# A hybrid attention and RG-LRU block on one core: the first round of attention scores moved into the last product of the input projection, the second unit's q loaded a round later

## The chip, the core and the metric

One core of one Trainium2 chip. The metric is device time in microseconds (us). The kernel before was run three times without a profile: median 2137.27 us, from 2135.4 to 2137.36. One more execution was profiled; the trace and all times inside the kernel come from it, counted from the start of its span.

## The reference, cut to what matters

A decoder block on x of 2048 positions by 1024 features, in float32. One input projection gives q, k and v for three head groups of eight heads, two SiLU gates, the RG-LRU input and two merge gates:

```python
proj = x @ w_in[l] + b_in[l]
q, k, v, g_attn, u_lru, g_lru, gate_logits = jnp.split(proj, SPLIT_POINTS, axis=-1)
```

The attention is banded: blocks of 128 queries against their own and the previous block of keys, the positions taken with stride 1, 4 or 16 by head group. For each block:

```python
s = jnp.einsum('brnqhd,brnkhd->brnhqk', qb, kw) * (Dh ** -0.5)
s = jnp.where(valid[None, None, :, None], s, NEG_INF)
m = jnp.max(s, axis=-1, keepdims=True)
p = jnp.exp(s - m)
l = jnp.sum(p, axis=-1, keepdims=True)
o = jnp.einsum('brnhqk,brnkhd->brnqhd', p, vw)
```

The three groups are combined by their denominators. The second branch is a causal convolution and a gated linear recurrence. Both are projected, weighted with sigmoid gates, summed, projected again and layer-normed with x.

## The kernel before, in words

The kernel has three stages. The change is at the seam of the first two.

**Stage A, the input projection.** Its work is a list of steps `plan`, each a pair of 128 output features over half of the positions. A step is seven products of the Strassen kind (eight for the first step); a product is twelve 128x512 matmuls that sum up in one PSUM bank, since each float32 operand is split into a high and a low part and three of the four part products are taken (`product`, L582). The loop at L898 numbers the products T. In each turn it lets `product` issue its matmuls, runs the events due at T, the `late` queue and the chains (short sequences of follow-up work, each with a lag and costs), and then `evacuate` takes the product out of its bank. Halfway through a product, after six matmuls, `run(pe_late)` (L600) issues TensorE work that others have put off. The last step is a pair of merge gates. Each of its totals starts an `mg_chain` (L369): ScalarE takes tanh in place of the tile y (L374) and issues its store to `mg_scr` from its own DMA queue (L376). A chain started in one turn gets to its tanh in the next turn, or in the loop behind the last turn (L917).

PSUM in stage A is pool `ps`: four banks of tag q for products, two of tag t for transposes of v, two of tag g for the recurrence gates. The operand blocks of x lie in the SBUF slots X0 to X5 (`XSLOT`, L117); T4, the operand of the last but two of the products, lies in X0.

**Stage B, the attention.** Twelve units, each two heads of one group, are worked in four rounds each, so 48 rounds i. Unit u needs a tile A of q (high and low part, two loads of 1 MB), a tile B of k (two loads of 512 KB, then split in parts by another engine) and, by group, a tile V of v (four loads of 512 KB). Unit 1's q, tile A1, lies in X0, where T4 was. Loads are issued by SyncE in the order in which the program writes them. For the first units this is done during the last products (L909 to L911: unit 0's k, unit 0's q, unit 1's k, `firstv` for V00, unit 1's q), then V20 and the whole of unit 2 (L1087), then by rounds (L1095 to L1101, two pieces a round).

A round i of the loop at L1091 issues: `scores(i)` (L952, 24 matmuls on 64 rows each, pairs side by side, into four banks of tag s); `peak` (L978, VectorE adds the mask and takes the extreme of each row); `expo` (L987, ScalarE's exponential in place, with the row sums); `turn` (L993, transposes of the probabilities of round i-1) and `bring` (L1003, their copies out of PSUM into tiles ptb, half by ScalarE and half by VectorE); `values` (L1018, of round i-2, TensorE) and `leave` (L1032, of round i-3, VectorE). Each engine works in the order written. Part of round i's exponentials are issued in round i+1.

**Stage C** has the two branch projections, the merge, the output projection and the norm.

**DMA semaphores.** The DMAs of SyncE and ScalarE together take eight completion semaphores in turn, DMAHW0 to DMAHW7. A DMA that takes one up waits on its own engine's queue for the DMA that had it before to land. Tiles of stage B lie where tiles of stage A lay, and the first to write there waits for those to be done with.

Of the kernel before, what the change touches and what calls it, by code (L numbers as in the profile page):

```python
# [8 lines left out]
F32 = mybir.dt.float32  # L9
# [22 lines left out]
def hybrid_block_kernel(ctx: ExitStack, tc: tile.TileContext, a: dict, out: bass.AP):  # L32
# [135 lines left out]
    def spend(**eng):  # L168
        for k, v in eng.items():
            left[k] = left.get(k, 0.0) - v  # L170
# [590 lines left out]
    def unit(u):  # L761

        return (0, 2, 1)[u % 3], u // 3

    def unit_parts(u):

        qs, ks = USLOT[u % 3]
        g, hp = unit(u)
        q = {n: qk_scr[n, 4 * g + hp] for n in ("qh", "ql", "k")}
        units[u] = [None, None]  # L770

        def k_part(j):
# [12 lines left out]
            def fn():  # L785
                if j == 0:
                    units[u][1] = big(ks, [P, 2, S], F32R, f"B{u}")
                sp.dma_start(flat(units[u][1][:, 1, cols]), q["k"][:, cols])
                for i in range(2):
                    c0 = (2 * j + i) * CH  # L790
                    later(3 + i if u < 2 else 1, lambda c0=c0: split(slice(c0, c0 + CH)))
            return fn

        def q_part(i, n):
            def fn():
                if i == 0:
                    units[u][0] = big(qs, [P, 2, S], F32R, f"A{u}")
                sp.dma_start(flat(units[u][0][:, i]), q[n])
            return fn

        return [k_part(0), k_part(1), q_part(0, "qh"), q_part(1, "ql")]
# [3 lines left out]
    def v_parts(g, j):  # L805
        src = v_scr[g][j]

        def part(i):
            def fn():
                if i == 0:  # L810
                    VT[g, j] = big(VSLOT[g, j], [P, 16, 256], F32, f"V{g}{j}")
                V = VT[g, j]
                if g == 0:
                    sp.dma_start(V[:, 4 * i:4 * i + 4], src[i * CH:(i + 1) * CH].rearrange("(n p) f -> p n f", p=P))
                elif g == 1:
                    sp.dma_start(V[:, 4 * i:4 * i + 4], src[i * CH:(i + 1) * CH].rearrange("(j r) f -> j r f", r=4))
                else:
                    sp.dma_start(V[:, 4 * i:4 * i + 4], src.rearrange("(i r) f -> i r f", r=16)[:, 4 * i:4 * i + 4])
            return fn

        return [part(i) for i in range(4)]
# [70 lines left out]
            at(t, lambda n=n, kk=kk: comb_part(n, kk))  # L892
    at(10, lambda: start_chain(scales()))

    first, second, third, firstv = unit_parts(0), unit_parts(1), unit_parts(2), v_parts(0, 0)
    low = NS
    where = [(s, j) for s in range(NQ) for j in range(ticks[s])]
    for T, (s, j) in enumerate(where):  # L898
        now["n"] = T
        for k in ("PE", "ACT", "DVE", "POOL"):  # L900
            left[k] = min(left[k], 0.0) + LEN
        if plan[s][2]:
            spend(**COST[plan[s][2][j]])
        product(s, j)
        for fn in events.pop(T, []):
            fn()
        run(late)
        run_chains()
        if s == NQ - 1:  # L909
            for fn in ((), first[:2], first[2:], second[:2], firstv, second[2:], ())[j]:  # L910
                fn()  # L911
        evacuate(s, j)
        low = min(low, len(vacant))
        if TRACE:
            print(T, s, j, plan[s][4], len(vacant), len(lo_vacant), len(chains), {k: round(v, 1) for k, v in left.items()})
# [17 lines left out]
    at_p = stB.enter_context(tc.tile_pool(name="at_p", bufs=2, reuse_waits="tile"))  # L933
    Y = stB.enter_context(tc.tile_pool(name="Y", bufs=1, reuse_waits="tile"))
    aps = stB.enter_context(tc.tile_pool(name="aps", bufs=2, space=PSUM, reuse_waits="tile"))
    def prev(g, n):
        if g == 0:
            return n - 1 if n >= 1 else None
        if g == 1:
            return n - 4 if n >= 4 else None  # L940
        return None

    st = {}

    sta, ot = {}, {}

    def first(i, j):
        u, q = divmod(i, 4)
        g, _ = unit(u)
        return 0 if prev(g, 4 * q + j) is not None else P  # L950

    def scores(i):  # L952
        u, q = divmod(i, 4)
        g, _ = unit(u)
        A, B = units[u]
        if q == 0:
            sta[u] = p_p.tile([P, 16, 4], F32, tag="sta", name=f"sta{u}", bufs=3)
            ot[u] = at_p.tile([P, S], F32, tag="ot", name=f"ot{u}")
        for w in range(2):
            s = st["s", i, w] = [aps.tile([P, 2, 256], F32, tag="s", name=f"s{i}{w}{h}", bufs=4) for h in range(2)]  # L960
            for j in range(2):
                n = 4 * q + 2 * w + j
                lo = first(i, 2 * w + j)
                for x, y in ((0, 0), (1, 0), (0, 1)):
                    for h, hs in enumerate(HALF):
                        K = B[hs, y]
                        if g == 2:
                            k = K.rearrange("p (c r j) -> p r c j", c=4, r=16)[:, n]
                        elif lo:
                            k = K[:, n * P:(n + 1) * P]  # L970
                        elif g == 0:
                            k = K[:, (n - 1) * P:(n + 1) * P]
                        else:
                            c, r = divmod(n, 4)
                            k = K[:, (c - 1) * CH:(c + 1) * CH].rearrange("p (c r j) -> p r c j", c=2, r=4)[:, r]
                        pe.matmul(s[h][:, j, lo:256], A[hs, x, n * P:(n + 1) * P], k, start=(x + y == 0), stop=(y == 1))  # L976

    def peak(i, j, h):  # L978
        u, q = divmod(i, 4)
        lo = first(i, j)  # L980
        if h == 0:
            st["p", i, j] = p_p.tile([P, 2, 256], F32, tag="p", name=f"p{i}{j}")
        dve.tensor_tensor_reduce(out=st["p", i, j][:, h, lo:256], in0=st["s", i, j // 2][h][:, j % 2, lo:256],  # L983
                                 in1=mask[:, lo:256], scale=1.0, scalar=3e38, op0=ALU.add, op1=ALU.min,
                                 accum_out=sta[u][:, 4 * q + j, h:h + 1])

    def expo(i, j, h):  # L987
        u, q = divmod(i, 4)
        p = st["p", i, j][:, h, first(i, j):256]
        s = sta[u][:, 4 * q + j]  # L990
        act.activation(p, p, AF.Exp, scale=-1.0, bias=s[:, h:h + 1], accum_out=s[:, 2 + h:3 + h])  # L991

    def turn(i, w):  # L993
        js = (2 * w, 2 * w + 1)
        pp = [st.pop(("p", i, j)) for j in js]
# [94 lines left out]
    loads = []  # L1090
    for i in range(NG + 3):  # L1091
        u = i // 4
        on, turns = i < NG, 0 < i <= NG
        run(late)
        if i in VORD:  # L1095
            loads += v_parts(*VORD[i])
        if i % 4 == 0 and 1 <= u <= 9:
            loads += unit_parts(u + 2)
        for _ in range(2):
            if loads:  # L1100
                loads.pop(0)()  # L1101
        if on:
            scores(i)
        if i > 2:
            leave(i - 3)
        if turns:
            expo(i - 1, 2, 1)
            expo(i - 1, 3, 0)
            expo(i - 1, 3, 1)
        if on:  # L1110
            peak(i, 0, 0)
            expo(i, 0, 0)
            for j, h in ((0, 1), (1, 0), (1, 1)):
                peak(i, j, h)
        if turns:
            turn(i - 1, 0)
            bring(i - 1, 0, 0, act)
            bring(i - 1, 0, 1, dve)
        if on:
            for j, h in ((0, 1), (1, 0), (1, 1)):  # L1120
                expo(i, j, h)
            peak(i, 2, 0)
            peak(i, 2, 1)
        if turns:
            turn(i - 1, 1)
            light = unit((i - 1) // 4)[0] == 2 or i % 3 == 0
            bring(i - 1, 1, 0, dve if light else act)
        if on:
            peak(i, 3, 0)
            peak(i, 3, 1)  # L1130
            expo(i, 2, 0)
        if turns:
            bring(i - 1, 1, 1, dve)
        if i > 1 and i - 2 < NG:
            values(i - 2)
        if i in (40, 41):
            prep_wl(i - 40, 2)
# [384 lines left out]
```

## Time and profile before

| | us |
|---|---|
| three runs, median | 2137.27 |
| the profiled execution, its own time | 2143.06 |
| its span | 2141.3 |
| TensorE busy | 2101.0 (98%) |
| VectorE busy | 1700.2 (79%) |
| ScalarE busy | 1080.3 (50%) |
| last product starts | 1463.28 |
| first score matmul | 1466.09 |
| first matmul of `values(0)` | 1477.81 |
| first matmul of `scores(4)` (unit 1) | 1485.85 |

The profiled execution's own time is 1.8 us over its span, and 5.8 us over the median of the runs. PE is TensorE, PEld its weight loads, DVE VectorE, ACT ScalarE, POOL GpSimd, SP SyncE; a q behind an engine is its sequencer, which issues DMAs. A row such as `q<-xB,hS` names what is written and read, with buffer numbers left out. A wait is put down to what ended last before the instruction went on.

### The profile page before, as it was taken

Reading aid. Unit: us, or ns where it says so; the run is one execution under the profiler, and the core shown is the slowest. Engines: PE = TensorE matmul, PEld = TensorE weight load, DVE = VectorE, ACT = ScalarE, POOL = GpSimd, SP = SyncE. Lnnn points to the kernel's source line nnn. Section 1 sums busy time; section 2 is a strip of 40 time slices with the busy share of each in tenths; the row PEclk is TensorE's granted clock in tenths of the full one; section 3 lists DMA queues with packets and bytes.
Section 4 is the critical chain, followed back from the end, with each engine's and each line's share of the span. In section 5 each row is a group of like instructions: output and inputs, shape, how many; then the busy total and the mean of one; then the engine's idle time right before and its main releaser. Section 6 shows DMA issues by size and latency. Waiting matters only on the chain.

```text
span 2141.3 us, 36029 instructions
## 1 busy us (share of the span) xinstructions
PE 2101.0 (98%) x12016; PEld 1749.0 (82%) x12016; DVE 1700.2 (79%) x3009; ACT 1080.3 (50%) x2284; POOL 736.5 (34%) x581
## 2 busy tenths in 40 slices
PE   8999999999999999999999999999999999999998
PEld 6888887888888788888888887888888888878887
DVE  8788988999979977787787886886999645466667
ACT  6354545457446565546557666557999411121100
POOL 1545454554654312121222221222535434322120
PEclk9999999999999999999999999999999999999999
DMA  8888887998998977777778788779898788874431
GB/s 269 257 261 251 255 255 224 270 280 245 286 270 251 302 228 203 227 221 218 248 244 276 254 260 253 241 229 373 303 305 254 219 275 280 283 251 160 165 108 69
DMA packets 348266, 525.74 MB, mean 246 GB/s; under 512 B 123568, under 2 KB 156336, under 8 KB 344240
## 3 DMA queue, kind: packets, MB, share of 16 engines
q1 hardware_dynamic: 330368, 491.64, 71.0%
q0 software_dynamic: 10080, 18.35, 5.4%
q10 hardware_dynamic: 7632, 13.44, 1.8%
q8 instruction: 96, 1.57, 0.3%
q14 instruction: 90, 0.74, 0.1%
HBM read 318.18 MB, written 190.45 MB: 238 GB/s over the span
## 4 chain that ended last, share of the span: by engine, by line
PE 82%; ACT 6%; DMA 5%; DVE 5%; issue 1%; SPq 1%; POOL 0%; DVEq 0%; ACTq 0%; POOLq 0%
PE q L597 59%; ACT p L991 4%; PE z L1388 3%; PE z L1386 3%; PE z L1387 3%; PE yb L1276 2%; PE yb L1277 2%; PE yb L1278 2%; PE o L1029 1%; PE ya L1354 1%; PE ya L1355 1%; PE ya L1356 1%; PE vtp L348 1%; ACT ptb L1014 1%; DMA yb_scr<-gB 1%
## 5 line engine op out<-in xcount | busy, mean ns | idle before, releaser
L597 PE MATMUL q<-xT,hS 128*128 128x512 f32 x1680 | 519.0, 390 | 0.4 <-DVE y L216 0.4
L597 PE MATMUL q<-xT,l 128*128 128x512 f32 x1120 | 436.0, 389 | 0.0
L597 PE MATMUL q<-xB,hA 128*128 128x512 f32 x1248 | 389.0, 393 | 6.0 <-ACT xB L204 5.7
L597 PEld LDWEIGHTS q<-xT,hS 128*128 128x128 f32 x1680 | 314.1, 188 | 65.4 <-issue 0.8
L597 PE MATMUL q<-xB,l 128*128 128x512 f32 x904 | 354.8, 392 | 1.9 <-DMA l<-wl_scr 1.8
L597 PEld LDWEIGHTS q<-xB,hA 128*128 128x128 f32 x1248 | 235.0, 189 | 56.1 <-ACT xB L204 5.7
L597 PEld LDWEIGHTS q<-xT,l 128*128 128x128 f32 x1120 | 210.2, 188 | 44.0
L597 PEld LDWEIGHTS q<-xB,l 128*128 128x128 f32 x904 | 171.1, 189 | 39.4 <-DMA l<-wl_scr 2.7
L216 POOL TENSOR_TENSOR S<-S,wA 128x512 f32<-128x512 f32 x35 | 45.7, 1305 | 418.9 <-DVE S L216 328.4
L216 POOL TENSOR_TENSOR sw<-sw,sin 128x512 f32<-128x512 f32 x96 | 160.7, 1679 | 72.0 <-DMA sw<-y 59.4
L261 ACT ACTIVATE hA<-wA 128x512 fp32r<-128x512 f32 x218 | 135.7, 624 | 90.3 <-DMA wA<-in_w_in_dram 43.0
L597 PE MATMUL q<-xB,hS 128*128 128x512 f32 x560 | 175.6, 395 | 3.0 <-DVE v L216 3.0
L991 ACT ACTIVATE p<-p,sta 128x256 f32<-128x256 f32 (+1 forms) x384 | 172.2, 455 | 5.9 <-DVE sta L983 5.2
L597 PE MATMUL q<-xT,hA 128*128 128x512 f32 x560 | 173.0, 390 | 1.5 <-DVE xT L205 0.9
L261 ACT ACTIVATE hS<-S 128x512 fp32r<-128x512 f32 x175 | 109.1, 623 | 99.2 <-DVE S L216 54.6
L216 POOL TENSOR_TENSOR l<-wA,hA 128x512 fp32r<-128x512 f32 x68 | 104.9, 1543 | 83.0 <-ACT hA L261 66.5
L597 PEld LDWEIGHTS q<-xB,hS 128*128 128x128 f32 x560 | 105.1, 190 | 25.0 <-issue 3.8
L597 PEld LDWEIGHTS q<-xT,hA 128*128 128x128 f32 x560 | 104.8, 188 | 24.6 <-DVE xT L205 1.3
L983 DVE CUSTOM_DVE_ANT_0 p<-s,mask 128x256 f32<-128x256 f32 (+1 forms) x384 | 118.7, 360 | 4.7 <-PE s L976 3.7
L216 DVE TENSOR_TENSOR y<-y,cos 128x512 f32<-128x512 f32 x96 | 108.8, 1139 | 14.8 <-DMA sw<-y 14.6
L1360 POOL TENSOR_TENSOR me<-gA,ybr 128x512 f32<-128x512 f32 x32 | 49.9, 1573 | 181.2 <-DVE gA L1359 119.6
L1388 PE MATMUL z<-wo,ml 128*128 128x512 f32 (+1 forms) x264 | 101.2, 383 | 0.9 <-DVE ml L1373 0.8
(201 smaller groups left out, 4423.7 us busy)
## 6 DMA issues: line engine op xcount, KB each, us to landing
wA<-in_w_in_dram SPq DMA_DIRECT2D x253, 256.0 KB, 5.0
wl_scr<-l SPq DMA_DIRECT2D x105, 512.0 KB, 4.9
l<-wl_scr SPq DMA_DIRECT2D x105, 512.0 KB, 4.8
sw<-y SPq DMA_DIRECT2D x384, 64.0 KB, 3.0
wS<-in_w_in_dram SPq DMA_DIRECT2D x70, 256.0 KB, 4.5
wS<-in_w_in_dram POOLq DMA_DIRECT2D x70, 256.0 KB, 6.3
qh_scr<-hi SPq DMA_DIRECT2D x48, 256.0 KB, 5.2
v_scr<-vs SPq DMA_DIRECT2D x48, 256.0 KB, 4.4
```

The lines of the kernel that those rows point to most:

```text
L216: eng.tensor_tensor(out=out, in0=in0, in1=in1, op=op)
L261: act.activation(h, r, AF.Copy)
L597: pe.matmul(bank, w[:, ks], x[:, kk, xx], start=(first and i == 0), stop=(last and i == 11))
L983: dve.tensor_tensor_reduce(out=st["p", i, j][:, h, lo:256], in0=st["s", i, j // 2][h][:, j % 2, lo:256], in1=mask[:, lo:256], scale=1.0, s ...
L991: act.activation(p, p, AF.Exp, scale=-1.0, bias=s[:, h:h + 1], accum_out=s[:, 2 + h:3 + h])
L1276: pe.matmul(yb, WL[f][:, 0, k], xx[:, 0], start=(k == 0), stop=False)
L1277: pe.matmul(yb, WL[f][:, 0, k], xx[:, 1], start=False, stop=False)
L1278: pe.matmul(yb, WL[f][:, 1, k], xx[:, 0], start=False, stop=(k == 7))
L1360: pool.tensor_tensor(out=ME[c][:, f], in0=ga, in1=yb, op=ALU.add)
L1386: pe.matmul(z, mh[:, k], w[:, 0, hs], start=(k == 0), stop=False)
L1387: pe.matmul(z, mh[:, k], w[:, 1, hs], start=False, stop=False)
L1388: pe.matmul(z, ml[:, k], w[:, 0, hs], start=False, stop=(k == 7))
```

## The change

`scores`, `peak`, `expo` and what they need are moved, as they are, ahead of the loop of stage A, with three differences for round 0. Its scores go into the banks of tags t and g of `ps`. Its probabilities are one tile p0 in slot X0, behind T4. Its row extremes and sums, sta0, are a tile of the constants' pool. `scores(0)` is put into the last product's `run(pe_late)`, and `first_round`, all eight peaks and exponentials of round 0, is issued right behind that product, ahead of that turn's chains. Stage B's loop starts its own scores at round 1. Unit 1's q can now be loaded into X0 only when round 0's probabilities have been transposed, and is issued near the end of round 1 in the program.

```diff
-    first, second, third, firstv = unit_parts(0), unit_parts(1), unit_parts(2), v_parts(0, 0)
+    st = {}
+    sta, ot = {}, {}
...
+    def scores(i):
+        u, q = divmod(i, 4)
+        g, _ = unit(u)
+        A, B = units[u]
+        if i == 0:
+            sta[u] = cst.tile([P, 16, 4], F32, name="sta0")
+            p0 = big("X0", [P, 4, 2, 256], F32, "p0")
+            for j in range(4):
+                st["p", i, j] = p0[:, j]
+        elif q == 0:
+            sta[u] = p_p.tile([P, 16, 4], F32, tag="sta", name=f"sta{u}", bufs=3)
+        for w in range(2):
+            if i:
+                s = [aps.tile([P, 2, 256], F32, tag="s", name=f"s{i}{w}{h}", bufs=4) for h in range(2)]
+            else:
+                s = [ps.tile([P, 2, 256], F32, tag="tg"[w], name=f"s{i}{w}{h}", bufs=2) for h in range(2)]
...
+    def first_round():
+        for j in range(4):
+            for h in range(2):
+                peak(0, j, h)
+                expo(0, j, h)
+
+    early_k, late_k, third, firstv = unit_parts(0), unit_parts(1), unit_parts(2), v_parts(0, 0)
...
+        if T == len(where) - 1:
+            pe_later(0, lambda: scores(0))
         product(s, j)
+        if T == len(where) - 1:
+            first_round()
...
-            for fn in ((), first[:2], first[2:], second[:2], firstv, second[2:], ())[j]:
+            for fn in ((), early_k[:2], early_k[2:], late_k[:2], firstv, (), ())[j]:
...
-        on, turns = i < NG, 0 < i <= NG
+        on, turns = 0 < i < NG, 0 < i <= NG
...
-        if turns:
+        if i > 1 and turns:
             expo(i - 1, 2, 1)
             expo(i - 1, 3, 0)
             expo(i - 1, 3, 1)
...
+        if i == 1:
+            for fn in late_k[2:]:
+                fn()
```

The order of SyncE's DMAs from V00 to V10, with the semaphores that each waits for. Before:

```order
L814 DMA V00_14283<-v_scr00_75 128x4x256 [waits DMAHW6_49]
L798 DMA A1_14309<-qh_scr8_105 128x2048 [waits DMAHW7_49,PE_49]
L798 DMA A1_14309<-ql_scr8_106 128x2048 [waits DMAHW0_49]
L818 DMA V20_14356<-v_scr20_79 128x1024 [waits DVE_49,DMAHW1_49,PE_49,Activation_49]
L818 DMA V20_14356<-v_scr20_79 128x1024 [waits DMAHW2_49]
L818 DMA V20_14356<-v_scr20_79 128x1024 [waits DMAHW3_49]
L818 DMA V20_14356<-v_scr20_79 128x1024 [waits DMAHW4_49]
L788 DMA B2_14361<-k_scr4_95 128x1024 [waits DMAHW5_49]
L788 DMA B2_14361<-k_scr4_95 128x1024 [waits DMAHW6_49]
L798 DMA A2_14364<-qh_scr4_93 128x2048 [waits DMAHW7_49,PE_49,Pool_49]
L798 DMA A2_14364<-ql_scr4_94 128x2048 [waits DMAHW0_49]
L816 DMA V10_14422<-v_scr10_77 128x1024 [waits DMAHW1_49]
```

And in the changed kernel, from B2's second half on:

```order
L788 DMA B2_14404<-k_scr4_95 128x1024 [waits DMAHW4_49]
L798 DMA A2_14407<-qh_scr4_93 128x2048 [waits DMAHW5_49,PE_49,Pool_49]
L798 DMA A2_14407<-ql_scr4_94 128x2048 [waits DMAHW6_49]
L816 DMA V10_14419<-v_scr10_77 128x1024 [waits DMAHW7_49]
L816 DMA V10_14419<-v_scr10_77 128x1024 [waits DMAHW0_49]
L798 DMA A1_14505<-qh_scr8_105 128x2048 [waits DMAHW1_49,PE_49,Activation_49]
L798 DMA A1_14505<-ql_scr8_106 128x2048 [waits DMAHW2_49]
L816 DMA V10_14419<-v_scr10_77 128x1024 [waits DMAHW3_49]
```

A1's two loads have moved from ahead of V20 to behind V20, B2, A2 and the first two parts of V10. A2's two loads now wait for the semaphores that the last two gate stores hold, as the next rows show.

ScalarE at the seam: y71_3 and y63_3 are the last two gate tiles, p the probabilities, ptb01 the copy of the second half of round 0's transposes. Before:

```order
L374 ACTIVATE y71_3_14312<-y71_3_14312,bh_195 128x512 [waits DVE_49]
L376 DMA mg_scr_73<-y71_3_14312 128x512 [waits DMAHW2_49,Activation_49]
L374 ACTIVATE y63_3_14334<-y63_3_14334,bh_195 128x512 [waits DVE_49]
L376 DMA mg_scr_73<-y63_3_14334 128x512 [waits DMAHW5_49,Activation_49]
L991 ACTIVATE p00_14397,sta0_14367<-p00_14397,sta0_14367 128x128 [waits DVE_49] x2
L991 ACTIVATE p01_14401,sta0_14367<-p01_14401,sta0_14367 128x256 [waits DVE_49] x2
```

And in the changed kernel:

```order
L958 ACTIVATE p0_14320,sta0_14319<-p0_14320,sta0_14319 128x128 [waits DVE_49] x2
L958 ACTIVATE p0_14320,sta0_14319<-p0_14320,sta0_14319 128x256 [waits DVE_49] x6
L374 ACTIVATE y71_3_14309<-y71_3_14309,bh_195 128x512
L376 DMA mg_scr_73<-y71_3_14309 128x512 [waits DMAHW5_49,Activation_49]
L374 ACTIVATE y63_3_14377<-y63_3_14377,bh_195 128x512 [waits DVE_49]
L376 DMA mg_scr_73<-y63_3_14377 128x512 [waits DMAHW6_49,Activation_49]
L958 ACTIVATE p10_14450,sta0_14319<-p10_14450,sta0_14319 128x256 [waits DVE_49]
L1032 ACTIVATE ptb00_14471<-pt000_14457 128x6x64 [waits PE_49]
L958 ACTIVATE p10_14450,sta0_14319<-p10_14450,sta0_14319 128x256 [waits DVE_49]
L958 ACTIVATE p11_14454,sta0_14319<-p11_14454,sta0_14319 128x256 [waits DVE_49] x2
L1032 ACTIVATE ptb01_14498<-pt010_14480 128x8x64 [waits DMAHW5_49,PE_49]
```

Both gate steps have moved behind the eight exponentials of round 0. The store of y71_3 holds DMAHW5 and that of y63_3 holds DMAHW6; ptb01's copy waits for the first to land (before, the same copy waited for DMAHW2, which y71_3's store held then).

TensorE at the end of the last product (q6), in the changed kernel, where rows of the scores in between are left out:

```order
L597 MATMUL q6_71_14312<-xB22_7342,l6_71_14237 128x512
L943 MATMUL s000_14321<-B0_14217,A0_14241 128x128
L943 MATMUL s001_14322<-B0_14217,A0_14241 128x128
...
L943 MATMUL s011_14336<-B0_14217,A0_14241 128x256
L597 MATMUL q6_71_14312<-xB22_7342,hS4_71_14259 128x512 x2
L597 MATMUL q6_71_14312<-xB22_7342,l6_71_14237 128x512
L597 MATMUL q6_71_14312<-xB22_7342,hS4_71_14259 128x512 x2
L597 MATMUL q6_71_14312<-xB22_7342,l6_71_14237 128x512
L943 MATMUL s100_14422<-B0_14217,A0_14241 128x256
```

Round 0's 24 score matmuls stand after the sixth of the product's twelve; before, they stood behind the twelfth, with round 1's behind them in both.

More of the change, by code (lines that the diff above doesn't have):

```diff
@@ L893, in hybrid_block_kernel, with prev, first @@
     at(10, lambda: start_chain(scales()))
-    first, second, third, firstv = unit_parts(0), unit_parts(1), unit_parts(2), v_parts(0, 0)
+    def prev(g, n):
+        if g == 0:
+            return n - 1 if n >= 1 else None
+        if g == 1:
+            return n - 4 if n >= 4 else None
+        return None
+    st = {}
+    sta, ot = {}, {}
+    def first(i, j):
+        u, q = divmod(i, 4)
+        g, _ = unit(u)
+        return 0 if prev(g, 4 * q + j) is not None else P
+    def scores(i):
+        u, q = divmod(i, 4)
+        g, _ = unit(u)
+        A, B = units[u]
[11 more added lines that the diff above has]
+                s = [ps.tile([P, 2, 256], F32, tag="tg"[w], name=f"s{i}{w}{h}", bufs=2) for h in range(2)]
+            st["s", i, w] = s
+            for j in range(2):
+                n = 4 * q + 2 * w + j
+                lo = first(i, 2 * w + j)
+                for x, y in ((0, 0), (1, 0), (0, 1)):
+                    for h, hs in enumerate(HALF):
+                        K = B[hs, y]
+                        if g == 2:
+                            k = K.rearrange("p (c r j) -> p r c j", c=4, r=16)[:, n]
+                        elif lo:
+                            k = K[:, n * P:(n + 1) * P]
+                        elif g == 0:
+                            k = K[:, (n - 1) * P:(n + 1) * P]
+                        else:
+                            c, r = divmod(n, 4)
+                            k = K[:, (c - 1) * CH:(c + 1) * CH].rearrange("p (c r j) -> p r c j", c=2, r=4)[:, r]
+                        pe.matmul(s[h][:, j, lo:256], A[hs, x, n * P:(n + 1) * P], k, start=(x + y == 0), stop=(y == 1))
@@ new lines, in peak, with expo @@
+    def peak(i, j, h):
+        u, q = divmod(i, 4)
+        lo = first(i, j)
+        if h == 0 and i:
+            st["p", i, j] = p_p.tile([P, 2, 256], F32, tag="p", name=f"p{i}{j}")
+        dve.tensor_tensor_reduce(out=st["p", i, j][:, h, lo:256], in0=st["s", i, j // 2][h][:, j % 2, lo:256],
+                                 in1=mask[:, lo:256], scale=1.0, scalar=3e38, op0=ALU.add, op1=ALU.min,
+                                 accum_out=sta[u][:, 4 * q + j, h:h + 1])
+    def expo(i, j, h):
+        u, q = divmod(i, 4)
+        p = st["p", i, j][:, h, first(i, j):256]
+        s = sta[u][:, 4 * q + j]
+        act.activation(p, p, AF.Exp, scale=-1.0, bias=s[:, h:h + 1], accum_out=s[:, 2 + h:3 + h])
@@ L935, in hybrid_block_kernel @@
     aps = stB.enter_context(tc.tile_pool(name="aps", bufs=2, space=PSUM, reuse_waits="tile"))
[L936 to L991, printed above, removed]
```

2 lines of the change are left out of this document (added).

## The prediction

> **What bounds the kernel now.** I start with the page's chain of work that ended last, its shares by engine:
>
> ```profile
> PE 82%; ACT 6%; DMA 5%; DVE 5%; issue 1%; SPq 1%; POOL 0%; DVEq 0%; ACTq 0%; POOLq 0%
> ```
>
> TensorE sets the end, so an edit counts for what it does to the time at which TensorE gets on. The seam that is changed is read next, in the timeline of TensorE (start, duration, line, tiles, count, idle before):
>
> ```profile
> 1463.28 0.62 PE L597 MATMUL q<-xB,hS 128*128 128x512 f32 x2
> ...
> 1465.77 0.39 PE L597 MATMUL q<-xB,l 128*128 128x512 f32 x1
> 1466.09 0.32 PE L976 MATMUL s<-B,A 64*128 64x128 f32 x1
> 1466.94 1.67 PE L976 MATMUL s<-B,A 64*128 64x128 f32 x23 [0.53 <-DVE y L216]
> ...
> 1477.81 2.98 PE L1029 MATMUL o<-ptb,V 128*64 128x128 f32 x28 [0.57 <-ACT ptb L1014]
> ...
> 1485.85 0.33 PE L976 MATMUL s<-B,A 64*128 64x128 f32 x2
> ```
>
> The last product's twelve matmuls start from 1463.28 to 1465.77, one in 0.226 us. Round 0's scores get going at 1466.94, once VectorE has emptied a bank, the first `values` at 1477.81, and at 1485.85 round 4 begins, the first that reads unit 1's q (tile A1). In between TensorE is held back by ScalarE, whose timeline says why:
>
> ```profile
> 1464.27 0.72 ACT L374 ACTIVATE y<-y,bh 128x512 f32<-128x512 f32 x1 [2.06 <-DVE y L216]
> 1465.03 0.38 ACTq L376 DMA_DIRECT2D mg_scr<-y  x1
> ...
> 1468.16 0.40 ACT L991 ACTIVATE p<-p,sta 128x128 f32<-128x128 f32 x1 [0.52 <-DVE sta L983]
> ...
> 1471.91 0.49 ACT L991 ACTIVATE p<-p,sta 128x256 f32<-128x256 f32 x1
> ...
> 1474.24 0.58 ACT L1014 ACTIVATE ptb<-pt 128x512 f32<-128x512 f32 x1
> ```
>
> From 1468.16 on ScalarE runs without an idle mark: eight exponentials of round 0 in 3.75 us, the ninth (round 1's first) at 1471.91, and the copy into ptb01 at 1474.24. A gate step (tanh and the issue of its store) takes 1464.27 to 1465.41, that is 1.14 us. After 1486 the waits of TensorE, up to 1680 where the rounds end, are these two and no others:
>
> ```profile
> PE o L1029 <- ACT ptb L1014: 13.2, 41, 0.6
> PE pt L1001 <- ACT p L991: 1.1, 5, 0.2
> ```
>
> None is on a DMA, so no slack waits there that would give a delay back. Last, the loads, as SyncE issues them (A: q, B: k, V: v):
>
> ```profile
> 1452.95 0.43 SPq L798 DMA_DIRECT2D A<-ql_scr  x1
> ...
> 1466.35 0.85 SPq L798 DMA_DIRECT2D A<-qh_scr  x1
> 1468.36 0.33 SPq L798 DMA_DIRECT2D A<-ql_scr  x1
> 1468.86 4.01 SPq L818 DMA_DIRECT2D V<-v_scr  x4
> 1475.56 0.80 SPq L788 DMA_DIRECT2D B<-k_scr  x2
> 1476.47 0.36 SPq L798 DMA_DIRECT2D A<-qh_scr  x1
> 1478.85 0.32 SPq L798 DMA_DIRECT2D A<-ql_scr  x1
> 1480.13 4.16 SPq L816 DMA_DIRECT2D V<-v_scr  x4
> ```
>
> A1 is issued at 1466.35 and 1468.36, then V20, B2, A2 and V10. The same loads with the time to landing in the last column, for those issued from 1476.4 on:
>
> ```profile
> V<-v_scr SPq DMA_DIRECT2D x4, 512.0 KB, 12.6
> A<-qh_scr SPq DMA_DIRECT2D x1, 1024.0 KB, 12.5
> A<-ql_scr SPq DMA_DIRECT2D x1, 1024.0 KB, 12.6
> ```
>
> And the stretches that the sums below use, with TensorE's busy time, its granted clock, the DMA engines' share and GB/s:
>
> ```profile
> 331.27:334.68 3.41, 2.75 (x7) 0.50 0.66 94
> 334.68:338.10 3.42, 3.42 (x12) 0.50 0.98 248
> 1474.73:1478.15 3.42, 2.27 (x39) 1.00 1.01 414
> 1478.15:1481.56 3.41, 3.41 (x34) 0.50 1.02 406
> 1466.30:1494.05 27.75, 24.83 (x396) 0.94 1.03 406
> ```
>
> The last row matters most: from 1466 to 1494 the 16 DMA engines have no free time. These loads are a queue that is paid by the byte.
>
> **The change, step by step.**
>
> *Scores inside the product: 0.* The 24 matmuls are moved, not removed. Six of the product's matmuls are 6 x 0.226 = 1.36 us, so the scores start at 1463.28 + 1.36 = 1464.64. They need A0's low half, by these rows (time to landing of A0's two halves) issued at 1452.95 and landed 10.7 later, at 1463.65, one microsecond ahead of need:
>
> ```profile
> A<-qh_scr SPq DMA_DIRECT2D x1, 1024.0 KB, 7.1
> A<-ql_scr SPq DMA_DIRECT2D x1, 1024.0 KB, 10.7
> ```
>
> The banks are those of the gates and transposes, idle by then. If the load were a microsecond or two later, the product would stand as long; nothing could be gained, so the bounds are 0 and +2, and I take 0.
>
> *Softmax of round 0 earlier: 0.* In the trace the first exponential starts 1.22 us after the scores get going (1468.16 - 1466.94); now at 1464.64 + 1.22 = 1465.86. Eight of them end at 1469.61. But two gate steps that stood before them now stand behind them: 2 x 1.14 = 2.28, and round 1's first exponential starts at 1471.89, against 1471.91. TensorE's idle time in this ramp was ScalarE's work, and that is all still there. VectorE does not set it: its gate total now waits behind the eight maxima, and ScalarE comes to it later still.
>
> *The gate store of y71_3, later: +3.4 on ScalarE.* Its issue moves from 1465.03 to 1469.61 + 0.76 = 1470.37. The order's waits show that ptb01's copy waits for this store to land, since ptb01's place was y71_3's. Minimum, median and maximum landing of such stores between 1454 and 1468:
>
> ```profile
> DMA to landing us min/median/max: 6.1/7.9/9.1
> ```
>
> So it lands between 1476.5 and 1479.5; I take 7.2, between the least and the median, hence 1477.6. ScalarE gets to ptb01 at 1471.89 + 2.33 = 1474.2 and stands 3.4 us, with the exponentials of round 1 behind it and VectorE's half of the same copy held too. `values(0)` needs the copy that follows; it goes from 1477.81 to 1481.2, and round 4 from 1485.85 to 1489.2. Bounds: 2.3 to 5.3.
>
> *A1 a round later: +8.2 at round 4, which hides the 3.4.* SyncE's new order is V00, V20, B2, A2, two of V10's four parts, then A1. Before, A1, V20, B2, A2 and those two parts were served in the order of issue, the second part being issued at 1481.41 (1480.13 and a third of the way to the fourth part at 1483.97) and landing 12.6 later, at 1494.0. Afterwards the same set is served with A1 last. The bytes are the same and the engines are full (share 1.03), so the last of the set lands at 1494.0 again, and now that is A1's low half. TensorE is there at 1489.2, stands 4.8 us, and round 4 is 1494.05 - 1485.85 = 8.2 late. The 3.4 lies inside and is not added. Both ends: A2's low half waits for the other gate store, issued one gate step later at 1471.5 and landed at 1478.7, so A1's low half, four issues of 0.4 behind, leaves at 1480.3. With the least time of any 1 MB row (7.1) it would land at 1487.4 and hold nobody; with the slowest gate store (9.1) and 12.6 it would land at 1494.8. I take 1494.0, since the bytes agree: at 1480.3 A2, V10's two parts and A1 itself are still to come, 5 MB or 5.24 million bytes, 12.9 us at 406 GB/s, and the end of B2 ahead of them.
>
> *The clock after that wait: +1.8.* After 1478.15 the granted clock was 0.50 for 3.41 us behind a stretch with TensorE busy 2.27 of 3.42; at 331.27 it was 0.50 for two stretches, 6.8 us. A wait of 4.8 us should bring one or two, with a part of them inside the wait. I take 4.2 us worked at half clock, between the two, which loses 2.1, less 0.3 that a round waits anyway (13.2 / 41): 1.8. Ends: 0, and 3.1 when nearly two whole stretches are worked at half. The half-clock stretch that exists already is ahead of the wait, so whatever becomes of it is swallowed. The Trainium skill (TensorE: Matmul & The Clock Gate, HAM oscillation) asks for no TensorE idle gap over about 3.4 us. By it the stretch after 1478.15 should not be throttled, the longest wait ahead of it being 0.57; the trace differs and decides. By that rule a wait of A1 under 3.4 us would cost nothing in clock, by the trace it would; the sum would then be the wait alone.
>
> *Everything behind.* V20, B2 and A2 have 2 MB less ahead of them and land 5 us earlier, where nobody waits for them. Unit 3's loads stand behind A1 in the turn of the completion semaphores and move by about a microsecond; units 1 and 2 are worked off before they are asked for. Nothing in rounds 4 to 50 waits for a DMA, so the delay reaches the end.
>
> Sum: 8.2 + 1.8 = **+10.0 us**. The profiled execution took 2143.06 (span 2141.3, and 1.8 around it), so 2153.1 there; the runs' median of 2137.27 is 5.8 below it, and the difference carries over: **2147.3**.
>
> **Rivals.**
>
> 1. *In time, and nothing gained.* A1's low half lands by 1486, because the loads share the engines instead of standing in line, and the gate store lands by 1474.2. Then only the ScalarE sum is left, 0: **2137.3**, not slower. It decides at a landing within about 6 us of issue. For it: 7.1 was seen once. Against: the loads issued from 1476.4 on took 12.5 and more.
> 2. *The gate store alone.* A1 lands between 1486 and 1489, and ScalarE's wait for ptb01 is all that shows: +3.4, **2140.7**.
> 3. *The ramp closes.* From 1466.30 to 1494.05 TensorE is idle for 27.75 - 24.83 = 2.9 us and loses 1.7 to the half clock. All 4.6 go if the gate steps do not stand in ScalarE's way: **2132.7**. ScalarE's unbroken row speaks against it.
> 4. *SyncE's queue runs dry.* A2 now waits for both late gate stores. What stands ahead of A2 keeps the engines fed until about 1494.0 - 12.9 = 1481.1; each microsecond that a store lands after that is one more for A1. With 3 us of it and the clock at its upper end (3.1): 8.2 + 3 + 3.1 = +14.3, **2151.6**. It needs a store that takes 9.6 us or more.
>
> **How the numbers follow.** Forecast 0.70, rivals 1 to 4: 0.08, 0.12, 0.02, 0.08. The forecast's own range is 2143.3 (A1 at 1492, no loss in clock) to 2149.7 (1494.8, clock 3.1). The range to hold 8 in 10 takes in rival 2 with its lower end and part of 4: 2139.5 to 2151.0. About 0.2%, 4.3 us, is what a measurement of this kernel can tell from no change. Rival 3 just reaches that: faster 0.02. Rivals 1 and 2 lie within it: same 0.19. The forecast and rival 4, less a hundredth at the forecast's low end: slower 0.79.
>
> **What would show it.** In the profile after: round 0's exponentials from about 1465.9; round 1's first still at 1472; ptb01's copy idle before it on a gate store; A1's low half landing near 1494; at round 4's scores a TensorE wait near 5 us on that load, then a stretch at clock 0.50. If A1 lands before round 4's scores ask for it, or its bytes overtake A2 and V10, the prediction is wrong.

## The result and the profile after

The changed kernel takes 2148.30 us (median of 6 runs, 2142.43 to 2151.17) against 2136.97 (6 runs, 2133.18 to 2139.46) for the kernel before on the same chip: ratio 1.0059, 95% interval 1.0046 to 1.0072, or 9.8 to 15.4 us more (12.6 by the ratio, 11.3 between the two medians). The forecast was 2147.3, which is +10.0.

The profiled execution took 2146.88 us, with a span of 2145.2. Its chain of work that ended last has these shares by engine:

```profile
PE 75%; DVE 8%; DMA 7%; ACT 6%; issue 2%; SPq 1%; POOL 0%; DVEq 0%; ACTq 0%; POOLq 0%
```

TensorE's part is 75% now, 82% before. To compare the seam, one thing must be taken out first. The last product starts at 1458.96 here and at 1463.28 before, although the change leaves stage A alone up to there. Most of these 4.32 us go with the clock: before's trace has clock 0.50 in stage A for 6.8 us from 331.27, as the prediction quoted, and once more here (us, TensorE busy, granted clock, DMA share, GB/s), and this one nowhere:

```profile
1307.48:1310.89 3.41, 3.41 (x9) 0.50 1.05 422
```

The clock is not all of it, as over all traces of this document the last product starts between 1456.14 and 1463.28. So all times at the seam are counted from that start, or set into before's time by adding 4.32. TensorE's timeline after (start, duration, line, tiles, count, idle before):

```profile
1458.96 0.61 PE L597 MATMUL q<-xB,hS 128*128 128x512 f32 x2
...
1460.42 1.67 PE L943 MATMUL s<-B,A 64*128 64x128 f32 x24
...
1474.60 2.06 PE L1019 MATMUL pt<-ident,p 64*128 64x64 f32 x16 [3.97 <-ACT p L958]
1477.05 3.25 PE L1047 MATMUL o<-ptb,V 128*64 128x128 f32 x28 [0.39 <-ACT ptb L1032]
...
1488.03 0.33 PE L943 MATMUL s<-B,A 64*128 64x128 f32 x2 [2.10 <-DMA A<-qh_scr]
1490.54 2.61 PE L943 MATMUL s<-B,A 64*128 64x128 f32 x22 [2.18 <-DMA A<-ql_scr]
...
1497.19 1.56 PE L943 MATMUL s<-B,A 64*128 64x128 f32 x24
```

The last row is round 5. From the start of the last product to it are 1497.19 - 1458.96 = 38.23 us; before, round 5 began here, 27.34 behind 1463.28:

```profile
1490.62 1.56 PE L976 MATMUL s<-B,A 64*128 64x128 f32 x24
```

So 10.9 us are lost in these rounds, and three rows of the changed kernel say where most of it is: TensorE stands 3.97 us in the ramp for ScalarE, and 2.10 + 2.18 at round 4 for the two halves of A1. From the last product's start to round 5 it is idle 7.6 us more than before (10.29 against 2.70), and the same work takes it 3.3 us longer (27.94 against 24.64), which is the half clock shown below. ScalarE's own timeline tells what the first of these is:

```profile
1461.74 0.40 ACT L958 ACTIVATE p<-p,sta 128x128 f32<-128x128 f32 x1 [3.85 <-DVE sta L950]
...
1465.48 0.71 ACT L374 ACTIVATE y<-y,bh 128x512 f32<-128x512 f32 x1
1466.22 0.33 ACTq L376 DMA_DIRECT2D mg_scr<-y  x1
...
1467.72 0.51 ACT L958 ACTIVATE p<-p,sta 128x256 f32<-128x256 f32 x1 [0.40 <-DVE ptb L1034]
...
1473.46 0.60 ACT L1032 ACTIVATE ptb<-pt 128x512 f32<-128x512 f32 x1 [3.29 <-DMA mg_scr<-y]
```

Both gate steps now stand behind the eight exponentials, and the copy into ptb01 waits 3.29 us for the store issued at 1466.22. The loads, as SyncE issues them:

```profile
1473.45 0.32 SPq L798 DMA_DIRECT2D A<-qh_scr  x1
1475.53 0.32 SPq L798 DMA_DIRECT2D A<-ql_scr  x1
1475.89 1.15 SPq L816 DMA_DIRECT2D V<-v_scr  x2
1477.15 0.50 SPq L798 DMA_DIRECT2D A<-qh_scr  x1
1477.69 0.44 SPq L798 DMA_DIRECT2D A<-ql_scr  x1
```

The first two are A2, the last two A1, whose times to landing (last column) are:

```profile
A<-qh_scr SPq DMA_DIRECT2D x1, 1024.0 KB, 10.7
A<-ql_scr SPq DMA_DIRECT2D x1, 1024.0 KB, 12.8
```

A1 lands at 1487.9 and 1490.5. Last, stretches of this execution with TensorE's busy time, its granted clock, the DMA share and GB/s:

```profile
1468.56:1471.97 3.41, 2.04 (x28) 1.00 1.02 386
1471.97:1482.21 10.24, 6.97 (x62) 0.50 0.97 368
...
1485.62:1489.03 3.41, 0.64 (x8) 1.00 1.00 406
1489.03:1495.86 6.83, 5.32 (x64) 0.50 1.04 420
```

With each long stand of TensorE comes half clock, a part of it within the stand itself: 10.24 us with the ramp's (1470.6 to 1474.6), 6.83 us with A1's (1485.9 to 1490.5).

### The profile page after: what moved, and what is told of

Same layout as the page of the kernel before. It is cut to its first block, busy times and chain, and to the rows that moved or that the text cites. A ratio compares the mean times of both kernels' runs of the same rounds, so it can differ in the third digit from the quotient of the medians.

```text
span 2145.2 us, 36023 instructions
## 1 busy us (share of the span) xinstructions
PE 2099.1 (98%) x12016; PEld 1749.2 (82%) x12016; DVE 1697.8 (79%) x3009; ACT 1080.5 (50%) x2284; POOL 735.8 (34%) x581
## 4 chain that ended last, share of the span: by engine, by line
PE 75%; DVE 8%; DMA 7%; ACT 6%; issue 2%; SPq 1%; POOL 0%; DVEq 0%; ACTq 0%; POOLq 0%
PE q L597 51%; ACT p L958 4%; PE z L1411 3%; PE z L1409 3%; PE z L1410 3%; PE yb L1299 2%; PE yb L1300 2%; PE yb L1301 2%; PE o L1047 1%; DMA wA<-in_w_in_dram 1%; ACT ptb L1032 1%; PE ya L1377 1%; PE ya L1378 1%; PE ya L1379 1%; PE s L943 1%
## 5 line engine op out<-in xcount | busy, mean ns | idle before, releaser
L958 ACT ACTIVATE p<-p,sta 128x256 f32<-128x256 f32 (+1 forms) x384 | 172.1, 454 | 15.5 <-DVE sta L950 14.5
L216 DVE TENSOR_TENSOR y<-y,cos 128x512 f32<-128x512 f32 x96 | 100.8, 1056 | 16.2 <-DMA sw<-y 16.1
```

The lines of the kernel that those rows point to most:

```text
L216: eng.tensor_tensor(out=out, in0=in0, in1=in1, op=op)
```

## The experiments

Three theories stood at first. **Load theory**: A1's late landing sets the time, and the rest hides beneath it. **Gate-store theory**: the store that ptb01 waits for costs it. **Product theory**: the scores inside the product do harm by themselves. Each kernel below is judged by two numbers: its median against runs of the kernel before on the same chip, and, from its trace, the time from the last product's start to round 5 ("R5": 27.34 in the profile of before, 38.23 after). A difference in us is taken from the ratio, as a share of the median of before; the two medians themselves lie up to 1.4 us away from it.

**e1_p0_x1.** The change without its load: p0 gets another slot, so A1 is loaded where it was.

```diff
-            p0 = big("X0", [P, 4, 2, 256], F32, "p0")
+            p0 = big("X1", [P, 4, 2, 256], F32, "p0")
...
-            for fn in ((), early_k[:2], early_k[2:], late_k[:2], firstv, (), ())[j]:
+            for fn in ((), early_k[:2], early_k[2:], late_k[:2], firstv, late_k[2:], ())[j]:
...
-    for fn in v_parts(2, 0) + third:
+    for fn in v_parts(2, 0) + third[2:]:
...
-            for fn in late_k[2:]:
+            for fn in third[:2]:
```

> The changed kernel, but round 0's probabilities lie in slot X1, so that A1 is loaded at its old place in SyncE's order; unit 2's k, which follows in X1, is issued in round 1 instead. Load theory (A1's late landing sets the time): no wait on A1, round 4's scores about 3.4 us late against before because the wait of ptb01's copy for the gate store now shows; +3.4 us against before (2.0 to 4.5). Gate-store theory (the store ahead of ptb01 costs the ten microseconds): +10. Product theory (the scores inside the product do): +10.

Measured: 2140.49, ratio 1.0021 (1.0010 to 1.0031), +4.5 us. TensorE's waits between 1440 and 1530:

```profile
PE pt L1019 <- ACT p L958: 4.1, 2, 3.9
PE o L1047 <- ACT ptb L1032: 3.5, 12, 0.6
PE s L943 <- DVE y L216: 0.7, 1, 0.7
PE s L943 <- DVE sta L950: 0.5, 1, 0.5
```

No wait on a load is left, and the ramp's wait, 3.9 us here and 3.97 after, now shows. R5 is 31.23. The larger part of the loss belongs to the load.

**e3_late_q.** The other way round: the kernel before, with nothing but A1 moved.

```diff
-            for fn in ((), first[:2], first[2:], second[:2], firstv, second[2:], ())[j]:
+            for fn in ((), first[:2], first[2:], second[:2], firstv, (), ())[j]:
...
+        if i == 1:
+            for fn in second[2:]:
+                fn()
```

> The kernel before with one edit: unit 1's two q loads are issued near the end of round 1, as in the change; scores, softmax and gate steps stay where they were. Load theory: A1's low half lands about 8.5 us after round 4's scores of before would have asked for it, TensorE waits there some 8.5 us, clock 0.50 behind it; +10 us against before (8.5 to 12). Gate-store theory and product theory: 0 (-1 to +1).

Measured: 2148.80, ratio 1.0060 (1.0044 to 1.0075), +12.8 us. Moving the load alone costs as much as the whole change. R5 is 38.30.

**e4_gate_first.** The changed kernel with the first round's softmax issued behind the chains, so that the store that ptb01 waits for goes out first.

```diff
-        if T == len(where) - 1:
-            first_round()
...
         run_chains()
+        if T == len(where) - 1:
+            first_round()
```

> The changed kernel, with round 0's maxima and exponentials issued behind that turn's chains, so that the tanh and the store of y71_3 go first. Load theory: ptb01's copy no longer waits for the store, the values of round 0 come 4 us earlier than in the changed kernel, and the time stays at +10 us against before (8.5 to 12) because the wait on A1 grows from 4.3 to about 8.5 us. Gate-store theory: at or below 0. Product theory: +10, without a longer wait on A1.

Measured: 2148.69, ratio 1.0057 (1.0045 to 1.0070), +12.2 us, nothing gained. Its waits in the same stretch:

```profile
PE s L943 <- DMA A<-qh_scr: 8.1, 1, 8.1
PE o L1047 <- ACT ptb L1032: 3.6, 10, 0.6
PE s L943 <- DMA A<-ql_scr: 1.9, 1, 1.9
PE s L943 <- DVE y L216: 0.7, 1, 0.7
PE s L943 <- DVE sta L950: 0.5, 1, 0.5
PE pt L1019 <- ACT p L958: 0.4, 2, 0.2
```

The ramp's wait is gone, and the wait for A1 has grown from 4.3 to 10.0 us. TensorE only came sooner to a load that lands when it lands: the 3.29 us that ptb01 stood for the gate store lay inside the wait for the load. R5 is 38.47.

**e5_q_ahead.** A1 at the place the change gave it, but issued ahead of A2 and V10.

```diff
-    for fn in v_parts(2, 0) + third:
+    for fn in v_parts(2, 0) + third[:2]:
...
-    VORD = {1: (1, 0), 17: (0, 1), 21: (2, 1), 25: (1, 1)}
+    VORD = {2: (1, 0), 17: (0, 1), 21: (2, 1), 25: (1, 1)}
...
-            for fn in late_k[2:]:
+            for fn in late_k[2:] + third[2:]:
```

> The changed kernel, with A1 ahead of A2's 2 MB and of V10 (whose parts start a round later), so 3 MB less stand in front of it. Load theory: A1's low half lands 7.7 us earlier than in the changed kernel (3 MB at 406 GB/s), round 4's scores wait under 1 us for it; the gate store's wait shows in its place: +3.4 us against before (2.0 to 5.0). Gate-store theory and product theory: +10.

Measured: 2140.52, ratio 1.0016 (1.0006 to 1.0026), +3.4 us. Counted from the last product's start, A1's halves are issued 3.5 and 2.3 us earlier than in the changed kernel (14.72 and 16.43 against 18.19 and 18.73) and no wait on them is left; R5 is 31.38, as in e1 (31.23).

**e7_v_ahead and e8_v_behind.** A dose: 1 MB of V10 more, or less, ahead of A1.

```diff
-        if i == 1:
+        if i == 2:
             for fn in late_k[2:]:
```

```diff
-    VORD = {1: (1, 0), 17: (0, 1), 21: (2, 1), 25: (1, 1)}
+    VORD = {2: (1, 0), 17: (0, 1), 21: (2, 1), 25: (1, 1)}
```

> The changed kernel with unit 1's q issued one round later still, behind all four parts of V10 instead of two: 1 MB more ahead of it. If the loads are a queue paid by the byte, A1's halves land 1.05 million bytes at 406 GB/s = 2.6 us later, TensorE's wait at round 4 grows from 4.3 to about 6.9 us, and the kernel takes 2.6 us more than the changed one: about +14 us over before (13 to 16). If the loads share the engines instead of standing in line, the landing moves by 1.3 us or less: +12.5. Gate-store and product theory: as the changed kernel, +11 to +12.5, with the wait for A1 longer but without effect.

> The changed kernel with V10 begun one round later, so that unit 1's q goes directly behind unit 2's: 1 MB less ahead of it. Queue paid by the byte: A1's halves land 2.6 us sooner, TensorE's wait at round 4 falls from 4.3 to about 1.7 us, and the kernel takes 2.6 us less than the changed one; if the half-clock stretch behind that wait goes with it, another 1.9 less: +6.5 to +9 us over before, about +8. Shared engines: the landing moves by 1.3 us or less, +10 to +11. Gate-store and product theory: as the changed kernel, +11 to +12.5.

Measured: e7 2151.43, ratio 1.0078 (1.0064 to 1.0092), +16.7 us; e8 2144.28, ratio 1.0045 (1.0032 to 1.0058), +9.6 us. Round 4 of e7 and of e8 in TensorE's timeline:

```profile
1488.88 0.47 PE L943 MATMUL s<-B,A 64*128 64x128 f32 x2 [5.84 <-DMA A<-qh_scr]
1491.27 2.61 PE L943 MATMUL s<-B,A 64*128 64x128 f32 x22 [1.91 <-DMA A<-ql_scr]
```

```profile
1484.12 0.33 PE L943 MATMUL s<-B,A 64*128 64x128 f32 x2 [0.40 <-DVE sta L950]
1487.63 1.45 PE L943 MATMUL s<-B,A 64*128 64x128 f32 x22 [3.18 <-DMA A<-ql_scr]
```

The last product started at 1456.14 in e7 and 1457.79 in e8. The low half's products therefore start 35.13, 31.58 (after: 1490.54 - 1458.96) and 29.84 us behind it: 1 MB more costs 3.5, 1 MB less gives 1.7, around the 2.6 of a pure queue. Both are more than the 1.3 or less expected of shared engines, and the spread between executions does not explain them: the changed kernel profiled again (e12, below) has 31.59 for the 31.58. In e8 the high half lands 26.2 us behind the last product's start (after: 28.9), 2.7 sooner as the queue has it, and the low half 3.6 behind that; in e7 the high half lands 3.5 us behind V10's last part, where the two halves of A1, of the same size, land 2.4 to 2.6 apart in after and e7. What takes the engines for that microsecond, in both kernels, was not found.

**e2_x1_gate_first.** e1's load with e4's order: both costs removed, the scores inside the product kept.

> The kernel of e1_p0_x1 (round 0's scores in a place of their own, A1 loaded where it was before the change) with the first round's softmax put behind the last tick's gate step, so that y71_3's tanh and store go first again. What is left of the change is the scores inside the product and the softmax one gate step earlier. In e1_p0_x1 round 5 began 3.9 us late by the trace (last product's start to round 5's scores: 31.23 against 27.34), all of it behind the wait of ptb01's copy for a gate store. Gate-store theory: that wait goes (no TensorE wait over 1 us between 1465 and 1500), and since only one gate step now stands between round 0's eight exponentials and round 1's first, the first values start about 1.0 us sooner after the last product's start than before (e4_gate_first: 13.57 against 14.53): 1.0 us faster than before, between -3 (if the half-clock stretch behind 1478 goes too) and +0.5. Product theory (the scores inside the product cost by themselves): +3.5 to +4.5 as in e1_p0_x1, with the first values no sooner than there.

Measured: 2133.48, ratio 0.9993 (0.9985 to 1.0002), -1.5 us (-3.2 to +0.4). Its seam:

```profile
1456.90 0.62 PE L597 MATMUL q<-xB,hS 128*128 128x512 f32 x2
...
1470.46 1.75 PE L1047 MATMUL o<-ptb,V 128*64 128x128 f32 x28 [0.57 <-ACT ptb L1032]
...
1481.91 1.56 PE L943 MATMUL s<-B,A 64*128 64x128 f32 x24
```

The first `values` come 13.56 us behind the last product's start, 0.97 sooner than before (14.53), and R5 is 25.01. The product theory, which had +3.5 to +4.5, is out: no cost of the scores inside the product shows. What they bring, with all else in order, is 0.97 us at the first `values`, nearly one gate step (1.14) on ScalarE.

**e6_q_ahead_gate_first.** e5's order of loads with e4's order of gate store and softmax.

> The kernel of e5_q_ahead (p0 in the place the change gave it, unit 1's q ahead of unit 2's q and of V10) with the first round's softmax behind the last tick's gate step. Load theory: A1 now stands where A2 stood in e4_gate_first, where A2's halves landed at 1480.5 and 1483.0 and TensorE was ready for round 4 at 1480.05; so it waits 2.5 to 3 us for A1, the low half's products start about 0.9 us late against before (1483.05 against 1485.85 less 3.67 of earlier stage A), and with none or one half-clock stretch behind it the time is +0.5 to +3 us over before, about +2. Gate-store theory alone (the loads no longer matter): -1 to 0, and no wait for A1. Product theory: +3.5 or more, without that wait.

Measured: 2141.82, ratio 1.0027 (1.0017 to 1.0037), +5.8 us, above what was expected. The waits, 1.16 and 2.02 us, were close to the 2.5 to 3 expected:

```profile
1480.16 0.33 PE L943 MATMUL s<-B,A 64*128 64x128 f32 x2 [1.16 <-DMA A<-qh_scr]
1482.50 1.49 PE L943 MATMUL s<-B,A 64*128 64x128 f32 x22 [2.02 <-DMA A<-ql_scr]
```

**e9_x1_gate_first_again and e10_q_ahead_gate_first_again.** The last two once more: one to tell a small gain from none, the other because its time did not fit its trace.

> The kernel of e2_x1_gate_first once more, to learn whether it is faster than before. In its trace round 5 began 2.3 us early (last product's start to round 5's scores: 25.01 against 27.34): 1.0 us by the first values coming sooner and the rest by the half-clock stretch that before had behind 1478 and this one has not. If that is the whole, 1.5 to 2.5 us faster. If before's half-clock stretch in the rounds comes in only some of its executions, the gain is nearer to 1.0 us and cannot be told from none.

> The kernel of e6_q_ahead_gate_first once more. In its trace round 5 began 2.4 us late, but its times were 5.8 us over before (3.6 to 7.9), which no other kernel shows: elsewhere the times lie within 2.5 us of the delay at round 5. If the delay at round 5 is all, +2.4 (1 to 4) and the first measurement was high by chance; if something behind round 5 costs too, +5 to +6 again, and the trace shows the offset grow between round 5 and the end of the rounds; if the half-clock stretch behind the wait differs from execution to execution, +4 with a delay at round 5 that is not 2.4.

Measured: e9 2133.26, ratio 0.9996 (0.9984 to 1.0008), -0.9 us, R5 25.01 again; e10 2138.23, ratio 1.0016 (1.0006 to 1.0026), +3.4 us, R5 29.58 (e6: 29.71). Nothing behind round 5 is seen to cost: from round 5 to the first product of stage C the traces of e6 and e10 take 190.11 and 190.06 us, that of before profiled again (e11) 190.01. So the first time of e6 was most likely high by chance. e2 is not shown to be faster than before; about 1 us is likely.

**e11_before_again and e12_after_again.** Both kernels profiled once more, to see which part of their clock belongs to the kernel.

> The kernel before, profiled once more, for its clock: is the half-clock stretch behind 1478, with no wait over 0.57 us ahead of it, part of every execution? If it is, the last product's start to round 5's scores takes 27.3 us again. If it comes in some executions only, the same stretch takes about 26.0 us (27.34 less the 1.3 us by which round 5 gained in e2_x1_gate_first beyond the 1.0 us of its first values), with no row at clock 0.50 between 1465 and 1500.

> The changed kernel, profiled once more, for the spread of its waits and clock. If the delay belongs to the order of loads and stores, the last product's start to round 5's scores takes 38.2 us again, within 1 us, with the waits on the load at round 4 adding up to 4 to 5 us and half clock behind both long waits of TensorE (ramp and round 4). If the clock is a matter of the execution, one of the two half-clock stretches is missing or a step of 3.4 us shorter, and the delay is 1 to 2 us less.

e11: R5 is 1485.05 - 1459.05 = 26.00, the second of the two cases, and from 1465 to 1500 its clock is full throughout. Three stretches, the second being the least busy:

```profile
1467.90:1471.31 3.41, 3.09 (x48) 1.00 1.03 425
1471.31:1474.73 3.42, 2.31 (x36) 1.00 0.98 381
1474.73:1478.14 3.41, 3.23 (x68) 1.00 1.03 413
```

The half-clock stretch that before's profile had behind 1478 thus comes in some executions only; two profiles can't say in how many. It was worth 1.3 us in that execution. e12: R5 38.94, waits on A1 of 3.10 + 2.00, clock 0.50 for 6.83 us behind the ramp's wait and 10.24 behind A1's. The delay repeats within 0.7 us, though the lengths of its two half-clock stretches are exchanged.

All measured, with R5 counted against 26.00, the R5 of e11:

| kernel | R5 - 26.00 | measured, us |
|---|---|---|
| after | +12.2 | +12.6 |
| e3, A1 moved alone | +12.3 | +12.8 |
| e4, gate store first | +12.5 | +12.2 |
| e7, 1 MB more ahead | +15.5 | +16.7 |
| e8, 1 MB less ahead | +9.6 | +9.6 |
| e1, A1 at its old place | +5.2 | +4.5 |
| e5, A1 ahead | +5.4 | +3.4 |
| e6, e10, A1 ahead, store first | +3.7, +3.6 | +5.8, +3.4 |
| e2, e9, both undone | -1.0, -1.0 | -1.5, -0.9 |

The rounds from 0 to 4 account for all times, to within the intervals of about 2 to 3 us each way. The times of e3, e4, e7 and e8 lie 0.2 to 0.8 us above the ranges that the load theory gave them, which is less than these intervals.

## Why the prediction was right, by its steps

- **Scores inside the product, 0: right.** They start 1.46 us behind the last product's start without a wait (forecast 1.36), and e2 shows no cost.
- **Softmax earlier, 0: right.** Round 1's first exponential starts 8.76 us behind the last product's start (1467.72 - 1458.96), against 8.63 before. All that was won was given back to the two gate steps. e2 and e9, with only one of them behind, gained 0.97 at the first `values`.
- **Gate store, +3.4 on ScalarE: right.** Its issue is 7.26 behind the last product's start (forecast 7.09), ptb01 stands 3.29, and the first `values` start 18.09 behind it against 14.53, +3.56. That it hides under the load is what e4 (nothing gained) and e1 (it shows) prove. By its trace it costs more alone than the 3.4 of rival 2, as half clock comes with that wait too: R5 is 5.2 over e11's in e1. The time of e1 (+4.5, from 2.1 to 6.6) can't tell the two apart.
- **A1, +8.2 at round 4: right in kind, 0.8 too small.** The low half's products start at 1490.54 + 4.32 = 1494.86 in before's time, against a forecast of 1494.05 and before's 1485.85: +9.0. The bytes did not agree quite: A2 is issued at 1473.45 and 1475.53, as the two gate stores land that hold it (issued at 1466.22 and 1467.35, landed 7.2 and 8.2 later, against 7.2 in the forecast for both), and the stretch around it moved 368 GB/s. In before's profile the same stretch, 4.32 later, moved 414:

```profile
1476.29:1486.53 10.24, 9.22 (x136) 0.83 1.03 414
```

  46 GB/s over 10.24 us are 0.47 MB, or 1.1 us of loading. Most of it is lost in one place: from 1474.80 to 1476.30, around the issue of A2's low half at 1475.53, the engines moved 172 GB/s and were busy 71% of the time. That fits rival 4, SyncE's queue running dry, in a small dose. The prediction had the queue fed until 1481.1; in before's time it thinned from 1479.1 on. The wait itself was 4.3, not 4.8, as the half clock in the ramp brought TensorE to round 4 a microsecond late.
- **The clock after that wait, +1.8: right, the closeness by luck.** From the low half's products to round 5 it took 6.65 us (1490.54 to 1497.19), before 4.77 (1485.85 to 1490.62): +1.9. The same rounds of e12 took 7.35, +2.6. The Trainium skill (TensorE: Matmul & The Clock Gate, HAM oscillation) asks for no TensorE idle gap over about 3.4 us. Shorter ones are not harmless here: in e8 one wait of 3.18 was followed by 3.41 us at clock 0.50, and in e6 and e10 waits of 1.16 and 2.02, and of 2.42, were as well.
- **Nothing recovered: right up to stage C.** The delay is 10.9 at round 5 and the same to the last of stage C's products into yb. Between those and the products into ya and z, from 1870 to 1925, the profiled execution got 2.6 us back. How much that stretch gives back against the profile of before differs between executions of one kernel (0.7 us in e12; 3.2 in e2 and 1.6 in e9), and the runs' medians do not show that gain.
- **The total.** +10.0 forecast, +11.3 between the medians. The forecast was made against a profile in which a half-clock stretch of 1.3 us stood in the very rounds that were changed. It was called swallowed by the wait, which is right for that execution; but with 2137.27 for the runs it was tacitly taken to be in all of them. Against e11's R5 the change costs 12.2; the interval of the runs, 9.8 to 15.4, holds 10.9 and 12.2 alike. The ends of the forecast's own range are not quite what its terms add up to: A1 at 1492 gives 2143.4, not 2143.3, and 1494.8 with 3.1 gives 2149.3, not 2149.7. Nothing else rests on them.

Of the rivals, "in time" and "the gate store alone" fell with A1's landing. "The ramp closes" was true of 1.0 us, once one gate step was out of ScalarE's way (e4, e2). Only in e2 and e9, where no wait for A1 follows, does it reach round 5, and their times do not show it for certain.

## What to carry to other kernels

A new tile's place costs what must wait for that place: here the scores were free, and the slot of their probabilities pushed a load behind 6 MB of others, which set the time. In a queue without free time ask how many bytes stand ahead of a load and when the first reader comes; order the loads by their readers' times (e5). When two delays lie on one path, undo both before judging either, and profile the kernel before twice where a clock that changes by itself lies in the stretch in question.

## What the runs showed of the hardware

Half clock came in whole steps of 3.41 us. Between 1460 and 1500 it always began behind a step in which TensorE was busy 2.27 us or less of 3.41 (before: the stretch quoted in the prediction; after: 2.04 and 0.64) and never behind one of 2.31 or more (e11). Below that it was not certain: the 2.25 of e10, the 2.16 of e6 and the 1.46 of e3 brought none in the next step. In e8, four steps in a row:

```profile
1478.81:1482.22 3.41, 3.22 (x66) 1.00 1.01 425
1482.22:1485.63 3.41, 1.84 (x30) 1.00 1.00 413
1485.63:1489.05 3.42, 1.42 (x26) 1.00 1.02 410
1489.05:1492.46 3.41, 3.41 (x52) 0.50 1.02 411
```

A step of 1.84 brought no half clock, the next of 1.42 did. That a step's busy share has a part in it is argued from such rows; no run changed it by itself, and with 2.27 bringing half clock in one trace and 2.25 none in another it can't be all. On the whole a longer stand goes with a longer half clock: 3.41 us behind 2.4 to 3.2 us of waiting (e6, e8, e10; in before behind no single wait over 0.57), 6.83 or 10.24 behind 3.8 to 9.7 (after, e1, e3, e5, e7, e8, e12), and 13.65 behind 10.0 (e4). Between 1460 and 1500 the full clock came back only behind a step with TensorE busy 3.08 us or more (3.08 in e8), though not behind every such step (3.32 in e12).

Loads of 1 MB took 10.7 and 12.8 us behind a full queue (A1 in after), and 5.9 (A1's high half in e5, issued 5.8 us behind the load before it):

```profile
A<-qh_scr SPq DMA_DIRECT2D x1, 1024.0 KB, 5.9
```
